# The beginning of a two-layer diffusion backbone: rows requested first, squared on ScalarE, and normalized beside the filter spectrum

## The chip, the cores and the metric

The kernel runs as one program on one core of a Trainium2 chip. A core has five engines with a queue of instructions each: TensorE (PE; its weight loads are listed as PEld), VectorE (DVE), ScalarE (ACT), GpSimd (POOL) and SyncE (SP). Each engine takes its own queue in order. SP does nothing but start transfers (DMA), and POOL starts others. The metric is the device time of one execution in microseconds (us), as the median of several.

## The reference

Two layers act on 1024 latent tokens and 256 context tokens of 1024 channels. Layer 0, cut to what matters here:

```python
sh1, sc1, g1, sh2, sc2, g2 = ada_mod(c, ada_w[i], ada_b[i])      # silu(c) @ w + b, six parts of 1024
u_lat = modulate(rms_norm(h_lat, norm1_g[i]), sh1, sc1)           # norm * (1 + sc1) + sh1
u_ctx = modulate(rms_norm(h_ctx, norm1_g[i]), csh1, csc1)
y_lat = mixer_ab(u_lat, *ab)      # p = u @ w_in; Fourier mixing of 512 channels, Hyena on the rest
h_lat = h_lat + g1 * y_lat
h_lat = h_lat + g2 * swiglu(modulate(rms_norm(h_lat, norm2_g[i]), sh2, sc2), ...)
```

Hyena's long convolutions use two filters for each sequence length. A small network (two sine layers) and a window make the raw filter, which is divided by the sum of its absolute values; then its spectrum is taken. None of that depends on the tokens, so filters, modulation and normalization are independent until the product with `w_in`. Layer 1 is a neighbourhood attention with a feed-forward part.

## The kernel before

Channels lie on the 128 partitions, tokens along the free axis: eight blocks (`b`) of channels, and pieces `pc` of 512 latent (0, 1) or 256 context tokens (2). Products keep float32 accuracy by splitting an operand into a rounded high and a low part (`split`: the high part is a copy on ACT, L349, the low one a subtraction on DVE, L351).

The program is written as Python generators that `run` advances in turn; each `next` emits some instructions. A planner then orders each engine's queue by its own simulated times, earlier-emitted work first where both could go. So the order of emission sets the order loosely, and the data and the free buffers set the rest. Tiles come from pools with a fixed number of buffers: 21 of 4 KB per partition (`S4`), 35 of 2 KB (`S2`), and small ones for temporaries and weights (`wh`, `wl`, `ws`, eight slots together for the matrices `mat`). A load into a pool is held in its queue until a buffer is free, and whatever stands behind it there waits too.

The generators of the beginning are:

- `filter_mlp`: the sine layers, on PE, DVE and ACT.
- `filter_raw` (`fr`): the third weight split (L696, L349, L351), then for each of four blocks the products on PE, multiplied on DVE by a window that SP has loaded (L720). It has three steps left when `run` comes to its loop over `fr`.
- `ada_first` (`ada1`): the first two of the six modulations (scale, then shift), as products of 16 weight tiles of 512 KB (`in_ada_k`, loaded by POOL). Eight tiles make the scale, eight the shift; each ends with a turn into columns (L514) and additions (L518, L521).
- `norms` (`ng`): ten loads of 512 KB rows of tokens (`in_x_row`), then the sum of squares of each row, then the root and its reciprocal, then a broadcast of the factors, then loads of the same tokens by channels (`in_ctx_t`, `in_x_t`, six ahead), then 24 blocks of `norm_block` (L623 on DVE, L625 on ACT, L626 on DVE). Odd rows are squared on DVE in one instruction with its sum, even rows on ACT.
- `spectrum_l`: eight steps for the first latent filter. It loads matrices (`in_ff_l`, by POOL), forms sums on DVE (L863 to L906), multiplies on PE and stores; `filter_sum` in it takes the absolute values (L745 to L749).

`in_proj` follows: 16 blocks of 128 outputs, each with a load of 512 KB of `w_in`, its split, 72 matmuls and, from the fifth, a short convolution on DVE (L978 to L982). Between blocks it advances other generators by a list of counts: the second filter, the context filters, and `late_groups`, in which modulations 2, 3 and 4 are made on DVE. One step of that (`ada_group`, 24 in all) loads two 256 KB halves of one weight block into `S2` buffers and reduces each against two conditionings (four instructions of L549, two of L551).

```python
for k, _ in enumerate(self.spectrum_l(0, raws["l"][0], self.cast_half)):
    if k < 3:
        next(ada1, None)
    else:
        drain(ada1)
    for _ in range(4):
        next(ng, None)
```

Of the kernel before, what the change touches and what calls it, by code (L numbers as in the profile page):

```python
# [10 lines left out]
F32 = mybir.dt.float32  # L11
F32R = mybir.dt.float32r
F16 = mybir.dt.float16
AF = mybir.ActivationFunctionType
ALU = mybir.AluOpType
AX = mybir.AxisListType.X
MUL, ADD, SUB, MAX, MIN = ALU.mult, ALU.add, ALU.subtract, ALU.max, ALU.min
# [241 lines left out]
class Builder:  # L259
# [273 lines left out]
    def ada_group(self, l, m, conds, where):  # L533

        nc, a = self.nc, self.a
        for nb in range(m * 8, m * 8 + 8):
            if where == "s2":
                st = [self.S2(), self.S2()]
                for j in (0, 1):
                    self.ld(st[j], a["ada_w"][l, nb, :, j * 512:(j + 1) * 512])  # L540
            else:
                t = self.mat(1024, F32) if where == "mat" else self.S4()
                (self.ld if where == "mat" else self.ldr)(t, a["ada_w"][l, nb])
                st = [t[:, :512], t[:, 512:]]
            for c in reversed(conds):
                half = self.pt.tile([P, 2], F32, tag="ah", name=self.nm("ah"))
                for j in (0, 1):
                    o = st[j] if c == 0 else self.T()
                    nc.vector.tensor_tensor_reduce(o, st[j], self.cond[c][j], 1.0, 0.0, MUL, ADD,  # L549
                                                   half[:, j:j + 1])  # L550
                nc.vector.tensor_tensor(self.ada[(l, c)][:, nb:nb + 1], half[:, 0:1], half[:, 1:2], ADD)  # L551
            yield
        sl = slice(m * 8, m * 8 + 8)
        for c in conds:
            t = self.ada[(l, c)]
            nc.vector.tensor_tensor(t[:, sl], t[:, sl], self.adab[:, l * 48 + m * 8:l * 48 + m * 8 + 8], ADD)
            if m in (1, 4):
                g = (0 if m == 1 else 2) + l
                nc.vector.scalar_tensor_tensor(t[:, sl], t[:, sl], 1.0, self.gs[:, g * 8:g * 8 + 8], op0=ADD, op1=MUL)
# [1813 lines left out]
    def run(self):  # L2373
        nc, a = self.nc, self.a
# [9 lines left out]
        def drain(g):  # L2384
            for _ in g:
                pass
# [3 lines left out]
        def norms():  # L2390
# [4 lines left out]
            yield  # L2395
            sq = self.C(10)
            for i, t in rows:
                if i % 2:
                    nc.vector.tensor_tensor_reduce(t, t, t, 1.0, 0.0, MUL, ADD, sq[:, i:i + 1])
                else:  # L2400
                    with self.follow(self.last_hi):
                        nc.scalar.activation(t, t, AF.Square, accum_out=sq[:, i:i + 1])
                yield
            nc.scalar.activation(sq, sq, AF.Sqrt, scale=1.0 / D, bias=self.eps)
            nc.vector.reciprocal(sq, sq)
# [1 line left out]
            for pc in PCS:  # L2407
                w = WID[pc]
                t = self.T()
                for j in range(w // P):  # L2410
                    i = OFF.get(pc, LAT) // P + j
# [31 lines left out]
        u = Act()  # L2443
        ng = norms()
# [3 lines left out]
        next(mlp)  # L2448
        next(fr)
        self.setup_late()  # L2450
        next(mlp)
        for _ in range(3):
            next(ada1)
# [2 lines left out]
            next(ada1)  # L2456
        with self.tc.issue_after(self.clamp), self.tc.issue_after(self.sin):
            next(fr)
        for _ in fr:
            next(ada1)  # L2460
        next(ng)
        for k, _ in enumerate(self.spectrum_l(0, raws["l"][0], self.cast_half)):
            if k < 3:
                next(ada1, None)
            else:
                drain(ada1)
            for _ in range(4):
                next(ng, None)
        self.held = True
        second = (x for g in (self.filter_raw("l", raws["l"], (1,)),  # L2470
                              self.spectrum_l(1, raws["l"][1], self.cast2)) for x in g)
        next(second)
        next(ng)
        next(second)
        drain(ng)
        ada = self.late_groups()
# [16 lines left out]
            yield from self.inverse_c(1, y)  # L2493

        fc, cc = four(), conv()
        self.in_proj(u, ((second, (3, 3, 3, 1)), (filt, (0,) * 7 + (2,)), (ada, (0, 0, 1) + (2,) * 11 + (1, 0))), fc, cc)
        self.held = False
        drain(second)
        drain(ada)
# [36 lines left out]
        u = None  # L2536
# [248 lines left out]
```

## Time and profile before

| what | value |
|---|---|
| median of 3 runs | 2913.51 us (2904.85 to 2915.74) |
| the profiled execution | 2907.72 us, span 2906.0 us |
| PE busy | 2785.5 us (96%) |
| DVE busy | 2070.6 us (71%) |
| ACT busy | 1312.4 us (45%) |
| mean rate of transfers | 193 GB/s |

The span is what the profile covers, from the first to the last instruction. A busy share is the time in which an engine had an instruction under way. A window's row gives, for one stretch of the span, its length, then for each engine the busy time and the number of instructions, then the granted clock of TensorE, the share of the transfer engines in use and the rate in GB/s. In the list of groups the last column is the idle time just before such instructions and what ended it. In the timeline the columns are start, duration, engine, line, operation, output and inputs, count, and in brackets the idle time before it. The list of waits gives for a waiter and a releaser the total, the number and the longest.

### The profile page before, as it was taken

The numbers are of one execution on the slowest core, as the hardware profiler recorded it, in microseconds if no ns is written. First come the engines' busy times: TensorE is split into PE (matmuls) and PEld (weight loads), VectorE is DVE, ScalarE is ACT, GpSimd is POOL, SyncE is SP. The second block draws the span as 40 slices with busy tenths as digits, with TensorE's granted clock in tenths as the row PEclk, the third lists the DMA queues.
The fourth block names the chain that finished last, engine by engine and source line by source line (L and its number), as shares of the span: only waits on it lengthen the run. The fifth ranks groups of instructions, "written<-read, shape, count | busy, mean of one in ns | idle before, by whom it ended". The sixth has DMA issues, their size and how long they took to land. (4 is left out here: it accounts for less than half of the span.)

```text
span 2906.0 us, 43708 instructions
## 1 busy us (share of the span) xinstructions
PE 2785.5 (96%) x15496; PEld 2329.1 (80%) x15496; DVE 2070.6 (71%) x3793; ACT 1312.4 (45%) x2253; POOL 535.5 (18%) x859
## 2 busy tenths in 40 slices
PE   7899898989999999999999999999999999999998
PEld 3587787778898888888888888888887788888886
DVE  6868797766787888966777536677678877764555
ACT  3433325443554333333455327777765443333433
POOL 2021134251011112222110002232221022111000
PEclk8899999999999999999999999999999999999999
DMA  8646445654556555659984436776856276434753
GB/s 295 202 146 188 156 154 176 212 185 163 201 186 207 191 199 195 224 183 330 310 308 150 138 128 152 178 194 180 244 187 216 89 256 224 153 109 160 237 189 131
DMA packets 302824, 561.54 MB, mean 193 GB/s; under 512 B 82568, under 2 KB 128842, under 8 KB 302606
## 3 DMA queue, kind: packets, MB, share of 16 engines
q1 hardware_dynamic: 241806, 375.73, 41.3%
q0 software_dynamic: 58496, 178.83, 17.4%
q10 hardware_dynamic: 2304, 4.20, 0.4%
q8 instruction: 122, 2.00, 0.3%
q14 instruction: 96, 0.79, 0.1%
HBM read 411.30 MB, written 119.80 MB: 183 GB/s over the span
## 5 line engine op out<-in xcount | busy, mean ns | idle before, releaser
L1796 PE MATMUL ps<-s,s 128*128 128x512 f32 x1956 | 483.6, 389 | 0.3 <-ACT s L349 0.3
L1796 PEld LDWEIGHTS ps<-s,s 128*128 128x128 f32 x1956 | 367.0, 188 | 77.6 <-ACT s L349 1.1
L345 PE MATMUL ps<-s,wh 128*128 128x256 f32 (+1 forms) x1684 | 386.5, 330 | 4.8 <-ACT wh L349 2.3
L345 PEld LDWEIGHTS ps<-s,wh 128*128 128x128 f32 x1684 | 285.3, 193 | 37.3 <-issue 3.0
L345 PE MATMUL pq<-s,wh 128*128 128x512 f32 (+1 forms) x940 | 287.7, 382 | 6.2 <-DVE s L2611 2.5
L351 DVE TENSOR_TENSOR wl<-ws,wh 128x1024 fp32r<-128x1024 f32 (+1 forms) x141 | 167.7, 1190 | 140.7 <-ACT wh L349 136.0
L1969 PE MATMUL ps<-s,s 128*128 128x512 f32 (+1 forms) x1000 | 259.8, 383 | 3.2 <-DVE s L351 3.1
L349 ACT CAST wh<-ws 128x1024 fp32r<-128x1024 f32 (+1 forms) x141 | 144.6, 1026 | 260.0 <-PE ps L345 139.8
L345 PE MATMUL ps<-s,wl 128*128 128x256 f32 (+1 forms) x842 | 259.8, 329 | 0.8 <-DVE wl L351 0.8
L349 ACT CAST s<-s 128x1024 fp32r<-128x1024 f32 (+2 forms) x188 | 170.2, 933 | 191.8 <-DMA s<-d 169.3
L345 PE MATMUL ps<-s,s 128*128 128x65 f16 (+4 forms) x2774 | 235.0, 238 | 17.8 <-ACT s L349 3.9
L351 DVE TENSOR_TENSOR s<-s,s 128x1024 fp32r<-128x1024 f32 (+2 forms) x166 | 188.2, 1164 | 53.6 <-ACT s L349 53.4
L1969 PEld LDWEIGHTS ps<-s,s 128*128 128x128 f32 x1000 | 184.4, 188 | 41.5 <-DVE s L351 5.1
L349 ACT CAST s<-t 128x512 fp32r<-128x512 f32 (+1 forms) x211 | 119.8, 583 | 207.0 <-PE ps L1796 68.4
L345 PEld LDWEIGHTS pq<-s,wh 128*128 128x128 f32 x940 | 171.3, 191 | 36.8 <-DVE s L626 2.8
L1796 PE MATMUL ps<-s,wh 128*128 128x512 f32 x600 | 187.9, 393 | 0.0
L351 DVE TENSOR_TENSOR s<-t,s 128x512 fp32r<-128x512 f32 (+1 forms) x211 | 135.8, 654 | 60.5 <-ACT s L349 36.7
L345 PE MATMUL pq<-s,wl 128*128 128x512 f32 (+1 forms) x470 | 178.1, 380 | 0.0
L345 PEld LDWEIGHTS ps<-s,wl 128*128 128x128 f32 x842 | 160.4, 192 | 16.7 <-DVE wl L351 1.0
L345 PEld LDWEIGHTS ps<-s,s 128*128 128x128 f32 (+1 forms) x854 | 131.0, 194 | 30.3 <-ACT s L349 5.2
L1969 PE MATMUL ps<-s 128*128 128x512 f32 (+1 forms) x500 | 150.6, 385 | 0.0
L336 POOL DMA_DIRECT2D d<-s x154 | 83.2, 542 | 355.2 <-DVE s L1605 112.8
(487 smaller groups left out, 5586.1 us busy)
## 6 DMA issues: line engine op xcount, KB each, us to landing
s<-d SPq DMA_DIRECT2D x283, 256.0 KB, 3.8
s<-in_down SPq DMA_DIRECT2D x150, 256.0 KB, 4.2
d<-s POOLq DMA_DIRECT2D x138, 256.0 KB, 3.5
s<-in_ada_w POOLq DMA_DIRECT2D x56, 512.0 KB, 5.0
d<-tk POOLq DMA_DIRECT2D x98, 256.0 KB, 4.2
ws<-in_up SPq DMA_DIRECT2D x44, 512.0 KB, 3.8
d<-g POOLq DMA_DIRECT2D x86, 256.0 KB, 3.2
ws<-in_gate SPq DMA_DIRECT2D x42, 512.0 KB, 3.7
```

The costliest lines, as they stand in the source:

```text
L336: self.last_ldr = self.nc.gpsimd.dma_start(out, in_).ins
L345: self.nc.tensor.matmul(o, l, r, start=st, stop=sp)
L349: self.last_hi = nc.scalar.copy(hi, src).ins
L351: self.last_lo = eng.tensor_tensor(lo, src, hi.bitcast(F32), SUB).ins
L1796: nc.tensor.matmul(ps, x[:, sl], y, start=first and j == 0 and x is wh and y is xh, stop=j == 3 and x is wl, skip_group_check=True)
L1969: m = nc.tensor.matmul(acc[j][:, c0:c1], x[:, sl], y[:, xs], start=first and k == 0, stop=last and k == 2, skip_group_check=True)
```

## The change

`ada_group` gets an inner function that loads one weight block. In the `s2` form (the one of `late_groups`) the first block of a group is loaded before the loop and each step loads the next block before it reduces its own; the other forms load as they did. In `norms` all ten rows are squared on ACT. In `run` the row loads are emitted right after `setup_late`, the first modulation is emitted whole ahead of the spectrum, and the row squares and later steps of `norms` are spread over the loop over `fr` (two each) and the spectrum (three for each of its steps, where four were). In `in_proj` the counts for `late_groups` begin at the first block (1, 1, 1, then nine times 2, then 1, 1, 1, 0) where they were 0, 0, 1, then eleven times 2, then 1, 0.

```diff
     def ada_group(self, l, m, conds, where):
         nc, a = self.nc, self.a
-        for nb in range(m * 8, m * 8 + 8):
+        def load(nb):
             if where == "s2":
                 st = [self.S2(), self.S2()]
                 for j in (0, 1):
                     self.ld(st[j], a["ada_w"][l, nb, :, j * 512:(j + 1) * 512])
-            else:
-                t = self.mat(1024, F32) if where == "mat" else self.S4()
-                (self.ld if where == "mat" else self.ldr)(t, a["ada_w"][l, nb])
-                st = [t[:, :512], t[:, 512:]]
+                return st
+            t = self.mat(1024, F32) if where == "mat" else self.S4()
+            (self.ld if where == "mat" else self.ldr)(t, a["ada_w"][l, nb])
+            return [t[:, :512], t[:, 512:]]
+
+        ready = [load(m * 8)] if where == "s2" else []
+        for nb in range(m * 8, m * 8 + 8):
+            if where != "s2" or nb < m * 8 + 7:
+                ready.append(load(nb + len(ready)))
+            st = ready.pop(0)
             for c in reversed(conds):
...
             for i, t in rows:
-                if i % 2:
-                    nc.vector.tensor_tensor_reduce(t, t, t, 1.0, 0.0, MUL, ADD, sq[:, i:i + 1])
-                else:
-                    with self.follow(self.last_hi):
-                        nc.scalar.activation(t, t, AF.Square, accum_out=sq[:, i:i + 1])
+                with self.follow(self.last_hi):
+                    nc.scalar.activation(t, t, AF.Square, accum_out=sq[:, i:i + 1])
                 yield
...
         self.setup_late()
+        next(ng)
         next(mlp)
...
-        for _ in fr:
+        for i, _ in enumerate(fr):
             next(ada1)
-        next(ng)
+            for _ in range(2 if i < 5 else 1):
+                next(ng)
+        drain(ada1)
         for k, _ in enumerate(self.spectrum_l(0, raws["l"][0], self.cast_half)):
-            if k < 3:
-                next(ada1, None)
-            else:
-                drain(ada1)
-            for _ in range(4):
+            for _ in range(3):
                 next(ng, None)
...
         next(second)
-        next(ng)
+        next(ng, None)
         next(second)
...
-        self.in_proj(u, ((second, (3, 3, 3, 1)), (filt, (0,) * 7 + (2,)), (ada, (0, 0, 1) + (2,) * 11 + (1, 0))), fc, cc)
+        self.in_proj(u, ((second, (3, 3, 3, 1)), (filt, (0,) * 7 + (2,)), (ada, (1, 1, 1) + (2,) * 9 + (1, 1, 1, 0))), fc, cc)
```

`follow(x)` puts the instructions of its block behind `x` in their engine's queue; `last_hi` is the latest high copy of `split` emitted by then.

## The prediction

> **What bounds the kernel now.** I read the page's engine shares first, then the table by windows with borders at the ends of the stages that the change touches, then for each stage the groups with the idle time before them and the timeline.
>
> ```profile
> span 2906.0 us, 43708 instructions
> PE 2785.5 (96%) x15496; PEld 2329.1 (80%) x15496; DVE 2070.6 (71%) x3793; ACT 1312.4 (45%) x2253; POOL 535.5 (18%) x859
> ...
> 21.00:50.00 29.00, 25.12 (x73) 10.94 (x71) 17.21 (x33) 4.75 (x9) 3.77 (x8) 0.82 1.06 401
> ...
> 53.00:76.00 23.00, 12.33 (x32) 6.74 (x31) 23.00 (x33) 19.57 (x31) 1.05 (x2) 0.72 0.37 125
> 76.00:91.00 15.00, 15.00 (x50) 9.41 (x50) 3.68 (x14) 6.70 (x16) 0.00 (x0) 0.74 0.11 36
> 91.00:141.00 50.00, 39.11 (x156) 27.73 (x156) 49.92 (x85) 24.67 (x43) 3.18 (x6) 0.86 0.81 267
> 141.00:180.00 39.00, 36.94 (x205) 31.64 (x204) 20.81 (x42) 10.63 (x22) 6.95 (x9) 1.00 0.31 104
> 180.00:340.00 160.00, 145.34 (x739) 120.97 (x738) 130.01 (x354) 56.62 (x118) 29.17 (x46) 0.96 0.56 178
> 340.00:460.00 120.00, 109.96 (x553) 92.20 (x551) 101.70 (x247) 35.57 (x65) 32.49 (x35) 0.94 0.47 147
> 460.00:2906.00 2446.00, 2381.82 (x13659) 2024.32 (x13658) 1712.56 (x2972) 1148.97 (x1945) 448.87 (x730) 0.99 0.60 194
> ```
>
> TensorE bounds the kernel as a whole: from 460 us on it is busy 2381.82 of 2446 us. So an edit ahead of 460 us is worth what it brings forward the point from which TensorE runs full, and time won there is kept behind it. The stages ahead have other limits. From 21 to 50 us the transfer engines are full (share 1.06, 401 GB/s). From 53 to 76 VectorE is busy every microsecond, from 91 to 141 for 49.92 of 50. Between them, from 76 to 91, it does 3.68 us of work. From 141 to 180 TensorE is the limit with 36.94 of 39. From 180 to 460, the rest of `in_proj`, TensorE idles 14.7 + 10.0 us and VectorE 30.0 + 18.3 us, and neither is the limit by itself: they wait for each other.
>
> **The change part by part.** First the rows, which are requested ahead of the windows now.
>
> ```profile
> 5.10 0.79 SPq L330 DMA_DIRECT2D c<-in_ada_b  x1
> ...
> 8.77 10.60 SPq L330 DMA_DIRECT2D s<-in_win_l  x8
> 20.89 16.08 SPq L330 DMA_DIRECT2D s<-in_x_row  x10
> ...
> s<-in_x_row SPq DMA_DIRECT2D x10, 512.0 KB, 12.4
> mat<-in_ff_l POOLq DMA_DIRECT2D x8, 512.0 KB, 4.7
> s<-in_win_l SPq DMA_DIRECT2D x8, 256.0 KB, 12.5
> ...
> 52.65 0.69 DVE L720 TENSOR_TENSOR s<-ps,s 128x512 f32<-128x512 f32 x1
> 54.93 1.88 PE L345 MATMUL ps<-mat,c 128*2 128x512 f32 x4
> ...
> L720 DVE TENSOR_TENSOR s<-ps,s 128x512 f32<-128x512 f32 x12 | 7.6, 682 | 10.3 <-PE ps L345 10.3
> ```
>
> SP's queue holds the two in the other order after the change. From the end of `in_ada_b` at 5.9 us the ten rows take 16.1 us to issue, to 22, and the last lands 12.4 us later, at 34. The eight windows, moved behind ten transfers, take 10.6 us more, to 32.6, and the last lands at 45.1. Its product (L720, 0.69 us) then ends near 46. Before, the last product ended at 53.3, not for want of windows but because VectorE waited 10.3 us for TensorE (its biggest wait in L720's main group, up to 53 us). TensorE's queue has the shift's weight tiles among the filter's products, and POOL could not load the last of those tiles while matrices of the spectrum held the slots. Emitted whole ahead of the spectrum, those tiles go ahead of the spectrum's matrices in POOL's queue. So the raw filter is complete 7 us earlier. Ends: 0, if the products still stand behind late tiles, and 10.3, the whole wait. I take 7, by the sum of issue and landing.
>
> The moved spectrum matrices have the price of a stall at worst of one landing, 4.7 us (the median of `in_ff_l` up to 110 us), and nothing if they land before the raw filter is complete; they are hidden by the 46 us that the other transfers need anyway. I take 0.
>
> A rule of the Trainium skill bears on this (DMA: Bandwidth & Descriptors, sections "Queues, rings and completion order" and "Issuing engines are not separate DMA queues"). Transfers of all issuing engines share the same 16 transfer engines, which take turns between the queues packet by packet. The full share of 1.06 agrees. By it SP's queue would have half of the rate while POOL's has work, and with an estimated 8.2 MB up to the last window at half of 401 GB/s would end at 41 instead of 45 us. It also speaks against the edit: order is all that the change alters, not the rate.
>
> ```profile
> L2399 DVE CUSTOM_DVE_ANT_0 s<-s 128x1024 f32<-128x1024 f32 x5 | 6.1, 1215 | 0.0
> L2402 ACT ACTIVATE s<-s 128x1024 f32<-128x1024 f32 x5 | 5.2, 1050 | 0.0
> L2402 ACT ACTIVATION_READ_ACCUMULATOR s<-s 128x1 f32 x5 | 0.9, 188 | 0.0
> ACT s L349 <- DVE tk L873: 23.2, 1, 23.2
> ```
>
> Second, the squares. Five leave VectorE, 5 x 1.215 = 6.1 us out of the full stretch around 53 to 76. Ten on ScalarE take 10 x (1.050 + 0.188) = 12.4 us. ScalarE idled 23.2 us in one piece ahead of the spectrum's first cast, which waited for sums (L873) of the spectrum, and with the rows landing up to 34 us the squares fit into that gap. What stands behind them in ScalarE's queue are the absolute values of the raw filter, which cannot begin before some products are done. Cost 0; if the rows landed 10 us later than worked out, the 12.4 us would end some 10 us into the spectrum's work and delay the absolute values by up to 4. The ends are -6.1 and +4; I take -6.
>
> Third, the hole in VectorE's work from 76 to 91.
>
> ```profile
> 86.12 6.26 SPq L330 DMA_DIRECT2D ws<-in_w_in  x3
> ...
> 90.80 1.23 DVE L351 TENSOR_TENSOR wl<-ws,wh 128x1024 fp32r<-128x1024 f32 x1 [5.70 <-ACT wh L349]
> 92.43 1.37 SPq L330 DMA_DIRECT2D s<-in_ctx_t  x3
> 94.41 0.23 DVE L518 TENSOR_TENSOR c<-ps,c 128x8 f32<-128x8 f32 x2
> ...
> 100.84 1.66 DVE L623 SCALAR_TENSOR_TENSOR t<-s,c,s 128x256 f32<-128x256 f32 x4
> ```
>
> VectorE idles there because the next things in its queue are not ready: the split of `w_in` (5.70 us, SP requested it only from 86.12 on), and the spectrum's sums, which follow. The 24 normalized blocks would have filled the hole, but the shift's columns came only at 94.41, the tokens by channels were requested at 92.43, and the first block starts at 100.84. In the changed order the row factors are ready some 30 us earlier, the shift too, and the blocks are emitted beside the spectrum's last steps. The hole is 15 - 3.68 = 11.3 us. Filled wholly it moves the end of the blocks by 11.3, not at all by 0. I take 5: the row of the split shows that a queue in order keeps such waits even where other work is ready.
>
> These three make 7 + 6 + 5 = 18 us at the end of the blocks (141 us before). TensorE has to take it up: it was busy 39.11 of 50 us from 91 to 141, partly at a granted clock of 0.86, so 10.9 us of its idle time there are free, and the rest must come from the idle time of 53 to 76 (10.7 us). I count 14 of the 18 as kept. Ends: 0 and the sum of the upper ends, 10.3 + 6.1 + 11.3 = 27.7.
>
> Fourth, the later modulations.
>
> ```profile
> L549 DVE CUSTOM_DVE_ANT_0 t<-s,s 128x512 f32<-128x512 f32 x48 | 37.1, 787 | 31.2 <-DMA s<-in_ada_w 28.7 <-ACT s L530 2.3
> L549 DVE CUSTOM_DVE_ANT_0 s<-s,s 128x512 f32<-128x512 f32 x48 | 35.0, 730 | 0.0
> L551 DVE TENSOR_TENSOR c<-ah 128x1 f32<-128x1 f32 x48 | 9.4, 199 | 0.1
> L549 DVE DVE_READ_ACCUMULATOR2_ANT ah<- 128x1 f32 x96 | 7.6, 79 | 0.0
> ...
> PE ps L345 <- DVE s L351: 5.4, 1, 5.4
> PE ps L345 <- DVE s L980: 3.5, 2, 2.5
> PE ps L345 <- DVE s L982: 2.8, 2, 2.0
> PE pq L345 <- DVE s L351: 2.4, 1, 2.4
> ```
>
> Over 180 to 460 us VectorE stood 28.7 us for the weight blocks, because each was requested in the step that reduces it. Splits and convolutions that TensorE needs stand behind that wait. Requested one step ahead, the loads land (about 5 us) during other work; what is left is the first step of each of the three groups, some 3 waits of the kind (28.7 over 15 waits, seen one by one, is 1.9 us each): 5.7 us. So 23 us of VectorE's 48.3 idle us in this stage, about half, go. TensorE's waits for VectorE in the fence sum to 14.1; half of it is 7, and I take 6. Ends: 0 and 14.1.
>
> A step costs VectorE (37.1 + 35.0 + 9.4 + 7.6)/24 = 3.7 us. Two steps move from the thirteenth and fourteenth block of `in_proj` to the first two: 7.4 us. If they land between 141 and 180, 18.2 idle us of VectorE cover them; if they land ahead of 141, in the full stretch, they cost up to 7.4, and they give up to as much back at the end. I take 0, ends -7.4 and +7.4. The prefetch holds two more of the 35 `S2` buffers, and the four with the conditionings are taken two blocks earlier; what that may do stands with the rivals.
>
> **Sum**: 2907.72 - 14 - 6 = 2887.7 against the profiled execution. The median of the three runs, 2913.51, lies 5.8 above it, which gives 2893.5. I predict the middle, 2890 us.
>
> **Rivals.**
>
> *The order gives nothing.* The first 50 us are bound by transfers whose bytes are the same; the windows are later by as much as the rows are earlier, and VectorE's blocks still follow the spectrum because its matrices or the tokens by channels arrive late. For it: the 401 GB/s, and the product of the last window at 46 us, later than the first three quarters of the products before. Against it: 11.3 us of hole and the 6.1 us off VectorE do not depend on transfers. Then only the squares and half of the fourth part are left, 6 + 3 = 9 us: about 2902.
>
> *The edit does little of what it says*: the planner takes what is ready by its own times, and places blocks and prefetched loads nearly where they were. For it: the shift's last products ran at 54.93 us, amid the spectrum, though they are emitted in its later steps. Then the time is that of before, 2910.
>
> *The buffers: slower.* An earlier load that waits for an `S2` buffer holds SP's queue, and the load of `w_in` is behind it.
>
> ```profile
> SPq L330 <- DVE wl L351: 55.9, 10, 11.8
> ...
> ws<-in_w_in SPq DMA_DIRECT2D x4, 512.0 KB, 5.1
> ...
> 130.20 0.33 SPq L330 DMA_DIRECT2D ws<-in_w_in  x1
> ...
> 141.84 1.05 ACT L349 CAST wh<-ws 128x1024 fp32r<-128x1024 f32 x1
> ```
>
> `w_in` was requested at 130.20 and used at 141.84; with 5.1 us to land it had 6.5 us to spare. SP's longest such wait up to 330 us is 11.8 us. A hold of that length costs TensorE 11.8 - 6.5 = 5.3 us for a block. With seven of the fifteen blocks that carry steps the price is 37 us, against 14 gained: 2907.7 + 37 - 14 = 2931. It decides from six blocks on (6 x 5.3 = 32, above 14 + 14.6). Against it: the planner starts a load when it believes a buffer free, and the hold needs it to be wrong again and again. In a sentence beside it: the Trainium skill (Perfetto Trace Analysis, "Optimization Strategy") reads a gap that repeats on the engine that should be full as a sign that buffers ran out; no run here shows it yet.
>
> **How the numbers follow.** Forecast 0.45 (2872 to 2902); the order gives nothing 0.22 (2898 to 2908); little of what it says 0.13 (2905 to 2917); the buffers 0.20 (2920 to 2945). From no change a measurement tells about 0.5%, 14.6 us, so faster is under 2899 and slower above 2928. Faster: nearly all of the first and a little of the second, 0.47. Slower: most of the last, 0.18, and some room for a planner's order that goes wrong later, 0.03 more. Same: the rest, 0.32. The range is 2868 (the sum with 27.7 and 14.1, 2866, is nearly its lower end) to 2928; what it leaves out is most of the last rival and a few in a hundred below. The forecast's own range is 2872 to 2902.
>
> **What would show it.** Ten squares on ScalarE between 25 and 45 us and none on VectorE; last L720 near 46 instead of 53.3; L518's second pair near 50 instead of 94; the first L623 before 90 and the last L626 near 125 instead of 141; VectorE busy more than 11 of 15 us where the hole was; the wait of L549 for `in_ada_w` under 8 us; the span from the end of `in_proj` on unchanged. Wrong it would be if the absolute values wait behind squares, if the first L623 still starts near 100, or if SP shows waits above 12 us ahead of `w_in` loads in the first blocks of `in_proj`.

## The result and the profile after

The change makes no difference that the measurement can tell: 2909.23 us against 2909.84 us (medians of 12 executions each), a ratio of 1.0001 with a 95% interval of 0.9989 to 1.0013. The forecast of 2890 us was wrong. The profiled execution took 2911.94 us, its span 2910.2 us.

The table by windows of the kernel after, with the borders of the prediction (length, busy time of TensorE, its weight loads, VectorE, ScalarE and POOL with counts, granted clock, share of the transfer engines, GB/s):

```profile
21.00:50.00 29.00, 16.65 (x44) 9.62 (x44) 11.16 (x22) 23.08 (x45) 1.06 (x2) 0.66 0.87 344
53.00:76.00 23.00, 21.25 (x56) 6.87 (x55) 16.99 (x23) 7.95 (x12) 4.23 (x8) 0.95 0.59 183
76.00:91.00 15.00, 14.79 (x54) 10.43 (x53) 6.92 (x15) 5.04 (x11) 0.00 (x0) 0.71 0.39 132
91.00:141.00 50.00, 33.26 (x126) 24.08 (x127) 48.21 (x86) 24.48 (x42) 3.18 (x6) 0.80 0.68 222
141.00:180.00 39.00, 33.64 (x174) 28.04 (x173) 28.06 (x64) 14.04 (x28) 6.96 (x8) 0.96 0.55 189
180.00:340.00 160.00, 145.91 (x732) 120.74 (x732) 124.89 (x324) 53.50 (x111) 28.14 (x45) 0.94 0.54 171
340.00:460.00 120.00, 115.05 (x586) 96.63 (x586) 100.76 (x250) 37.54 (x68) 30.65 (x36) 0.97 0.44 138
```

VectorE did 17.21 us of work from 21 to 50 before and does 11.16 now. From 53 to 76, where it was full before, it is idle 6 of 23 us. VectorE's work has moved later, not earlier. Its timeline says why (start, duration, engine, line, operation, output and inputs, count, and in brackets the idle time before and what ended it; lines behind `ada_group` stand 7 higher than before, so L727 is the old L720, L630 and L633 the old L623 and L626):

```profile
43.76 0.22 DVE L2409 RECIPROCAL c<-c 128x10 f32<-128x10 f32 x1 [17.46 <-ACT c L2408]
43.89 0.64 DVE L727 TENSOR_TENSOR s<-ps,s 128x512 f32<-128x512 f32 x1
...
58.88 1.29 DVE L727 TENSOR_TENSOR s<-ps,s 128x512 f32<-128x512 f32 x2 [7.94 <-PE ps L345]
...
68.69 1.28 DVE L727 TENSOR_TENSOR s<-ps,s 128x512 f32<-128x512 f32 x2
...
80.26 0.24 DVE L518 TENSOR_TENSOR c<-ps,c 128x8 f32<-128x8 f32 x2 [1.34 <-PE ps L345]
87.23 0.88 DVE L630 SCALAR_TENSOR_TENSOR tk<-s,c,s 128x256 f32<-128x256 f32 x2 [6.73 <-DMA s<-in_ctx_t]
...
142.96 0.74 DVE L633 SCALAR_TENSOR_TENSOR s<-t,c,s 128x512 fp32r<-128x512 f32 x1
```

The reciprocal of the row factors stands in VectorE's queue ahead of the first product of the raw filter and waits 17.46 us for ScalarE. The first product starts at 43.89 (31.02 before, the line below), the last pair at 68.69 (52.65). The blocks begin at 87.23, as forecast ahead of 90, but the last one ends at 143.7 (141.1 before). In the kernel before:

```profile
31.02 0.69 DVE L720 TENSOR_TENSOR s<-ps,s 128x512 f32<-128x512 f32 x1 [2.92 <-PE ps L345]
```

The other three queues of the beginning in the kernel after, ScalarE, SP and TensorE, one after the other:

```profile
25.24 1.05 ACT L2406 ACTIVATE s<-s 128x1024 f32<-128x1024 f32 x1
...
40.02 1.06 ACT L2406 ACTIVATE s<-s 128x1024 f32<-128x1024 f32 x1 [1.37 <-DMA s<-in_x_row]
40.98 0.19 ACT L2406 ACTIVATION_READ_ACCUMULATOR s<-s 128x1 f32 x1
41.07 1.04 ACT L511 COPY g<-ps 2x512 f32<-2x512 f32 x2
42.12 1.28 ACT L2408 ACT_TABLE_LOAD   x1
```

```profile
6.37 14.48 SPq L330 DMA_DIRECT2D s<-in_x_row  x10
23.04 0.33 SPq L330 DMA_DIRECT2D c<-in_skip  x1
25.53 0.33 SPq L330 DMA_DIRECT2D c<-in_conv  x1
28.02 14.11 SPq L330 DMA_DIRECT2D s<-in_win_l  x8
83.73 0.33 SPq L330 DMA_DIRECT2D d<-s  x1
84.11 0.43 SPq L330 DMA_DIRECT2D s<-in_ctx_t  x1
```

```profile
41.68 2.08 PE L345 MATMUL ps<-s,s 128*128 128x512 f32 x4 [7.56 <-ACT g L511]
...
50.15 8.03 PE L345 MATMUL ps<-mat,c 128*2 128x512 f32 x14
...
75.50 2.93 PE L345 MATMUL ps<-s,mat 128*128 128x512 f32 x6
```

The ten squares run on ScalarE from 25.24 to 41.2, as forecast, but the copies of the first modulation (L511), the table for the root and the root itself stand behind them, and TensorE waits 7.56 us for those copies. SP issues nothing from 42.1 to 83.73: the token loads stand behind stores of the spectrum, and the spectrum's first product on TensorE comes at 75.50 (53.34 before). The waits of VectorE for ScalarE's `w_in` copies and for the modulation's weights, from 180 to 460 us (total, number, longest), before and after:

```profile
DVE t L549 <- DMA s<-in_ada_w: 28.7, 15, 6.9
DVE wl L351 <- ACT wh L349: 8.4, 4, 2.9
```

```profile
DVE wl L351 <- ACT wh L349: 22.1, 9, 6.4
DVE t L556 <- DMA s<-in_ada_w: 14.0, 8, 5.1
```

14.7 us of the wait for the weights went and 13.7 us of the wait for the copies came.

### The profile page after: what moved, and what is told of

It reads as the page before. It is cut to its first block, busy times and chain, and to the rows that moved or that the text cites. A ratio compares the mean times of both kernels' runs of the same rounds, so it can differ in the third digit from the quotient of the medians.

```text
span 2910.2 us, 43750 instructions
## 1 busy us (share of the span) xinstructions
PE 2787.2 (96%) x15496; PEld 2330.4 (80%) x15496; DVE 2063.2 (71%) x3783; ACT 1319.1 (45%) x2263; POOL 534.7 (18%) x859
## 5 line engine op out<-in xcount | busy, mean ns | idle before, releaser
L345 PEld LDWEIGHTS ps<-s,wh 128*128 128x128 f32 x1684 | 286.6, 193 | 37.1 <-issue 4.0
L1976 PEld LDWEIGHTS ps<-s,s 128*128 128x128 f32 x1000 | 184.6, 188 | 41.1 <-DVE s L351 4.5
L351 DVE TENSOR_TENSOR s<-t,s 128x512 fp32r<-128x512 f32 (+1 forms) x214 | 137.8, 655 | 60.6 <-ACT s L349 35.9
```

Of the source, the lines that this page charges most:

```text
L345: self.nc.tensor.matmul(o, l, r, start=st, stop=sp)
L351: self.last_lo = eng.tensor_tensor(lo, src, hi.bitcast(F32), SUB).ins
L1976: m = nc.tensor.matmul(acc[j][:, c0:c1], x[:, sl], y[:, xs], start=first and k == 0, stop=last and k == 2, skip_group_check=True)
```

## The experiments

Nothing of the computation is left out in any of them. Every time is a median; ratios are to the kernel before on the same chip, with 95% intervals. From each trace five marks are read, in us: the first and the last product of the raw filter and the first spectrum product (their starts), the end of the last normalized block, and the first turn of the inverse stage (the start of the first matmul of L1159, L1166 with the new `ada_group`), which stands where `in_proj` ends.

| kernel | first, last product | first spectrum product | last block ends | first turn | us | ratio |
|---|---|---|---|---|---|---|
| before | 31.0, 52.7 | 53.3 | 141.1 | 462.0 | | 1 |
| the change | 43.9, 68.7 | 75.5 | 143.7 | 469.7 | 2909.23 | 1.0001 (0.9989 to 1.0013) |
| late_only | 31.1, 52.8 | 53.5 | 141.2 | 465.8 | 2906.10 | 0.9997 (0.9986 to 1.0007) |
| begin_only | 42.5, 67.4 | 74.1 | 142.1 | 468.4 | 2908.85 | 1.0005 (0.9994 to 1.0017) |
| prefetch_only | 31.6, 53.5 | 54.2 | 142.0 | 462.9 | 2903.37 | 0.9985 (0.9977 to 0.9994) |
| squares_only | 31.8, 51.1 | 51.8 | 137.8 | 460.5 | 2902.06 | 0.9986 (0.9977 to 0.9995) |
| squares_prefetch | 31.1, 50.3 | 51.3 | 136.8 | 459.8 | 2907.65 | 1.0001 (0.9991 to 1.0011) |
| rows_first_only | 40.8, 64.4 | 66.6 | 155.3 | 479.6 | 2919.71 | 1.0041 (1.0026 to 1.0056) |
| drain_only | 31.8, 54.4 | 55.0 | 141.1 | 465.9 | 2909.82 | 1.0008 (0.9996 to 1.0020) |
| begin_root_late | 41.1, 68.3 | 72.2 | 141.4 | 466.9 | 2907.59 | 0.9997 (0.9988 to 1.0006) |
| windows_first | 33.0, 55.2 | 78.7 | 145.7 | 475.1 | 2917.38 | 1.0031 (1.0019 to 1.0042) |
| windows_tokens | 32.3, 54.6 | 78.1 | 136.2 | 466.8 | 2907.97 | 1.0002 (0.9992 to 1.0012) |
| windows_prefetch | 33.1, 55.4 | 78.9 | 145.7 | 472.1 | 2918.18 | 1.0038 (1.0025 to 1.0052) |
| factors_behind | 31.4, 56.5 | 57.2 | 138.2 | 461.3 | 2901.14 | 0.9972 (0.9961 to 0.9983) |
| after_factors_behind | 44.2, 67.9 | 69.2 | 143.4 | 462.6 | 2908.69 | 1.0006 (0.9997 to 1.0015) |
| factors_prefetch | 33.0, 55.6 | 56.3 | 137.3 | 458.9 | 2901.24 | 0.9989 (0.9975 to 1.0003) |

### The two halves

late_only is the kernel before with the new `ada_group` and the new counts of `in_proj`; begin_only is the changed kernel with both as before.

```diff
-            else:
...
+        ready = [load(m * 8)] if where == "s2" else []
...
-        self.in_proj(u, ((second, (3, 3, 3, 1)), (filt, (0,) * 7 + (2,)), (ada, (0, 0, 1) + (2,) * 11 + (1, 0))), fc, cc)
+        self.in_proj(u, ((second, (3, 3, 3, 1)), (filt, (0,) * 7 + (2,)), (ada, (1, 1, 1) + (2,) * 9 + (1, 1, 1, 0))), fc, cc)
```

> The kernel before, with the weight blocks of the later modulations loaded one step ahead and their steps begun at the first block of the input projection; the beginning is as it was. Theory A (two halves of opposite sign: the late part gains, the beginning loses as much): VectorE's wait for these blocks falls from 28.7 to about 14 us, the first turn of the inverse stage comes at about 452 to 456 us instead of 461.8, and the time falls by 6 to 10 us against the kernel before. Theory B (neither half does anything that reaches the end; VectorE's waits only change their names): the turn comes within 3 us of 461.8 and the time within 3 us.

> The changed beginning alone (rows first, all squares on ScalarE, first modulation emitted whole, normalization spread), with the later modulations as before. Theory A: VectorE stands some 17 us ahead of the reciprocal of the row roots with the filter's products queued behind it, the first spectrum matmul comes near 75 us instead of 53, the first turn of the inverse stage at about 470 to 477 us instead of 461.8, and the time rises by 6 to 13 us. Theory B: the turn within 3 us of 461.8 and the time within 3 us.

Measured: neither half changes the time by what the measurement can tell (0.9997 and 1.0005). So it is not a gain of one half that the other cancels. In both traces the first turn comes later than before, by 3.8 and 6.4 us, and the times do not show it. Each half was taken apart.

### The later half: the prefetch alone

prefetch_only has the new `ada_group` and the old counts.

> Only the load one step ahead; the steps are spread over the input projection as before. If the load ahead carries the gain of the late part (theory A1), the wait falls to about 14 us and the time is within 2 us of that of the late part alone. If the earlier begin of the steps carries it (A2), the time is within 2 us of the kernel before.

Measured: 0.9985, about 4 us, where late_only, with the earlier counts, has 0.9997. VectorE's wait for the weights falls to 10.6 us. These are its longest waits from 180 to 460 us now:

```profile
DVE wl L351 <- ACT wh L349: 23.9, 7, 7.6
DVE t L556 <- DMA s<-in_ada_w: 10.6, 5, 5.1
DVE s L351 <- DMA d<-s: 4.1, 1, 4.1
```

The three make 38.6 us; before, the two of the first fence above made 37.1. So VectorE hardly waits less, it waits for something else: the high copy of `w_in` above all. TensorE's busy time from 180 to 460 us rises by 1.1 us (146.45 + 109.99 against 255.30). The 4 us of the median are real by the interval, but the trace of one execution does not show where they arise. The earlier counts bring no gain of their own, and with them this one is gone.

### The beginning: one part at a time

squares_only squares all rows on ScalarE and changes nothing else; squares_prefetch adds the new `ada_group` to it.

```diff
-                if i % 2:
-                    nc.vector.tensor_tensor_reduce(t, t, t, 1.0, 0.0, MUL, ADD, sq[:, i:i + 1])
-                else:
-                    with self.follow(self.last_hi):
-                        nc.scalar.activation(t, t, AF.Square, accum_out=sq[:, i:i + 1])
+                with self.follow(self.last_hi):
+                    nc.scalar.activation(t, t, AF.Square, accum_out=sq[:, i:i + 1])
```

> The kernel before with all ten row squares on ScalarE and nothing else. If VectorE's work from 53 to 76 us sets the pace there (as I forecast), 6 us less of it brings the first normalized block from 100.8 to about 95 us and the time falls by 3 to 6 us. If what sets the pace there is the arrival of operands for TensorE and the order of the queues, ScalarE, busy 19.6 of 23 us in that stretch, becomes the limit with 6 us more, and the time stays within 3 us or rises.

> The two parts that gained by themselves, together: all squares on ScalarE and the load one step ahead, with the order of emission and the counts as before. If the two are independent the time falls by 4.3 + 3.7, near 8 us (ratio 0.997). If the planner's order is what made each of them gain, the sum is less, 2 to 5 us.

Measured: the squares alone bring 0.9986 and end the blocks 3.3 us earlier. Together with the prefetch they bring nothing (1.0001), though the blocks end a further 1.0 us earlier. Two gains of 0.15%, each beyond its interval, do not add.

rows_first_only requests the rows ahead of the windows and leaves the rest as before.

```diff
         self.setup_late()
+        next(ng)
         next(mlp)
...
-        next(ng)
         for k, _ in enumerate(self.spectrum_l(0, raws["l"][0], self.cast_half)):
```

> The kernel before with the row loads emitted ahead of the windows and nothing else; odd rows are squared on VectorE as before. Theory D: the windows land 10 us or more later and the products with them, first product near 40 us instead of 31, the first turn 2 to 5 us later than 461.8. Theory C: without the reciprocal in front of the products the later windows cost nothing at the end; the first turn within 2 us of 461.8.

Measured: slower by 0.41%, about 12 us. The first product starts 9.8 us later, the last 11.8, the first spectrum product 13.3, the last block ends 14.2 later and the first turn comes 17.6 later. But the late windows are not the only cause. The odd rows are still squared on VectorE, and the planner put these squares among the sine layers of `filter_mlp`, where VectorE waits 11.6 us for rows:

```profile
21.16 1.22 DVE L2399 CUSTOM_DVE_ANT_0 s<-s 128x1024 f32<-128x1024 f32 x1 [9.06 <-DMA s<-in_x_row]
...
38.17 1.29 DVE L351 TENSOR_TENSOR s<-t,s 128x512 fp32r<-128x512 f32 x2
...
40.78 0.69 DVE L720 TENSOR_TENSOR s<-ps,s 128x512 f32<-128x512 f32 x1 [0.16 <-DMA s<-in_win_l]
```

The weight split of the raw filter comes at 38.17 (26.80 before), and the first product waits only 0.16 us more for its window. So this run does not price the late windows by themselves.

drain_only ends the first modulation ahead of the spectrum.

```diff
+        drain(ada1)
         for k, _ in enumerate(self.spectrum_l(0, raws["l"][0], self.cast_half)):
-            if k < 3:
-                next(ada1, None)
-            else:
-                drain(ada1)
```

> The kernel before with the first modulation emitted whole ahead of the spectrum and nothing else. If its place matters, the shift's columns come well before 94 us and the first normalized block before 98 instead of 100.8, with the time 2 to 4 us lower. If what holds the blocks is the request of the tokens by channels, the first block stays at 100 us or later and the time within 2 us.

Measured: nothing (1.0008). The last of its 16 weight tiles is requested at 24.2 us (49.3 before), the second pair of L518 comes at 63.19 instead of 94.41, and the first block still starts at 100.85 (100.84 before). So the blocks had not waited for the shift's columns. And TensorE shows what the products had waited for. VectorE's longest wait for it in the kernel before, TensorE in that kernel, and TensorE in drain_only:

```profile
46.46 2.48 DVE L720 TENSOR_TENSOR s<-ps,s 128x512 f32<-128x512 f32 x4 [7.41 <-PE ps L345]
```

```profile
36.53 9.23 PE L345 MATMUL ps<-mat,c 128*2 128x512 f32 x18
```

```profile
36.26 8.75 PE L345 MATMUL ps<-mat,c 128*2 128x512 f32 x20
44.93 1.20 PE L345 MATMUL ps<-s,s 128*128 128x512 f32 x4
```

With its weights long requested, the modulation still holds TensorE for 8.75 us (9.23 for 18 such products before), and VectorE's waits for TensorE in this group sum to 11.0 us (10.3 before). So the wait of 7.41 us was for TensorE's own work, not for late tiles.

### Where the chain of row factors stands

The row factors need rows, squares on ScalarE, a table load and a root there, the reciprocal on VectorE, diagonals on ScalarE and a broadcast on TensorE. begin_root_late is begin_only with the reciprocal placed behind the products in VectorE's queue.

```diff
-                        nc.vector.tensor_tensor(t, ps, w, MUL)
+                        self.last_raw = nc.vector.tensor_tensor(t, ps, w, MUL).ins
...
-            nc.vector.reciprocal(sq, sq)
+            with self.follow(self.last_raw):
+                nc.vector.reciprocal(sq, sq)
```

> The changed beginning alone, with one more order: the reciprocal of the row roots stands behind the latest product of the raw filter in VectorE's queue. Theory C (the reciprocal, queued ahead of the products, is what delays the beginning): VectorE's wait of 14.9 us goes, the first product starts before 38 us, the first spectrum matmul comes near 65 us instead of 74, the first turn of the inverse stage near 461 instead of 468.4. Theory D (the windows, issued behind the rows, and the scale's copies, queued behind the squares on ScalarE, hold the products anyway): the first product still starts after 40 us and the first turn stays within 3 us of 468.4.

Its VectorE timeline:

```profile
41.08 0.69 DVE L720 TENSOR_TENSOR s<-ps,s 128x512 f32<-128x512 f32 x1 [13.81 <-DMA s<-in_win_l]
```

The first product now waits for a window instead, until 41.08. In begin_only, the kernel to compare with, the reciprocal waits 14.95 us and the first product starts at 42.48. So the wait for the root covered one for the window that is nearly as long: the reciprocal by itself costs 42.48 - 41.08 = 1.4 us there, the rest is the windows. Theory D holds; the last product (68.3) is no earlier than in begin_only, and the time stays (0.9997).

So the windows were given back. windows_first leaves the order of the loads as before and emits 13 steps of `norms` (loads, squares, root, broadcast) between the products and the spectrum; windows_tokens emits 14, so that the first six token loads are requested ahead of the spectrum's stores; windows_prefetch adds the new `ada_group`.

```diff
-        for _ in fr:
+        for i, _ in enumerate(fr):
             next(ada1)
-        next(ng)
+        for _ in range(13):
+            next(ng)
+        drain(ada1)
...
-            for _ in range(4):
+            for _ in range(3):
                 next(ng, None)
```

> The changed beginning alone, with one part undone: the rows are requested behind the windows again, as in the kernel before (so their squares, all on ScalarE, are emitted behind the raw filter too); the first modulation is still whole ahead of the spectrum and the normalization spread beside it. Theory E (the request of the rows ahead of the windows is what takes the rest of the change's gain): the first product comes near 31 us and the last near 54, as before; the first normalized block near 85 us, the last near 130 instead of 141, and the time falls by 5 to 10 us. Theory F (the other parts gain nothing that TensorE can use, whatever the order of the requests): the last block within 4 us of 141 and the time within 4 us.

> The same, and the first tokens by channels are requested one emission step earlier, ahead of the spectrum's first stores in SP's queue. If the stores in front of these requests are what holds the normalized blocks (VectorE waited 6.6 us for them in the changed beginning), the first block comes another 8 us or more earlier and the time falls by 2 to 4 us more. If the blocks wait for the shift's columns or the row factors, both stay as in the run without it.

> The changed beginning with the windows first, and the weight blocks of the later modulations loaded one step ahead with the counts as before: the parts of the change that did not lose. If gains of the beginning and of the load ahead add, the time is 3 to 4 us below that of the run without the load ahead. If, as with the squares, they do not, it is the same or higher.

Measured: windows_first is slower by 0.31%, against every expectation of it. Its products are nearly on time (33.0 to 55.2), but the spectrum comes at 78.7. TensorE and VectorE show the new hold:

```profile
71.93 1.22 PE L345 MATMUL pq<-t,c 128*128 128x256 f32 x2 [16.76 <-ACT t L2409]
73.10 2.08 PE L345 MATMUL pq<-tk,c 128*128 128x512 f32 x2
```

```profile
70.88 0.22 DVE L2402 RECIPROCAL c<-c 128x10 f32<-128x10 f32 x1 [4.33 <-ACT c L2401]
71.01 0.63 DVE L863 TENSOR_TENSOR t<-s 128x512 f32<-128x512 f32 x1
```

The broadcast of the factors stands ahead of the spectrum on TensorE and waits 16.76 us; on VectorE the spectrum's first sums (L863, at 37.02 before) stand behind the reciprocal. Requesting the tokens ahead of the stores (windows_tokens) brings the end of the blocks from 145.7 to 136.2 and the ratio from 1.0031 to 1.0002, with the spectrum still at 78.1: the token loads behind the stores are a second hold. The prefetch brings nothing here (1.0038).

factors_behind moves only the chain: 11 steps (loads and squares) ahead of the spectrum, the root and all that follows from its second step on.

```diff
-        for _ in range(13):
+        for _ in range(11):
             next(ng)
         drain(ada1)
         for k, _ in enumerate(self.spectrum_l(0, raws["l"][0], self.cast_half)):
-            for _ in range(3):
+            for _ in range(3 if k else 0):
                 next(ng, None)
```

> windows_first with one thing moved: ahead of the spectrum stand only the ten row loads and the ten squares (eleven steps of the normalization); the root, the broadcast and everything behind them are emitted from the spectrum's second step on, three steps to each. The filter's windows, the shift tiles ahead of the spectrum and the order of the loads stay as in windows_first. Theory Q (the chain of row factors, emitted ahead of the spectrum, is what holds the spectrum in the queues of ACT, DVE and PE): the first product of the spectrum on PE comes back from 78.72 us to between 53 and 60, the reciprocal no longer stands on DVE ahead of the spectrum's sums, and the time is 5 to 12 us below that of windows_first, 2905 to 2912 us, a ratio to before of 0.999 to 1.0015. Rival R (not the factors: the squares on ACT, or the shift tiles emitted ahead of the spectrum, hold it): the first product of the spectrum stays behind 70 us and the ratio stays near 1.003. Rival S (the spectrum comes back but the time does not follow it, because the tokens requested behind the spectrum's stores hold the last blocks): first product of the spectrum under 60, last normalized block still at 144 to 147 us, ratio still near 1.003.

Measured: 0.9972, 16 us below windows_first and 8 us below before; the two intervals are far apart. The spectrum is back at 57.16, the reciprocal stands at 75.38 among the spectrum's splits and waits 0.92 us, the blocks start at 83.39 and end at 138.2, and the first turn comes 13.8 us earlier than in windows_first (461.3 against 475.1). Theory Q holds, and the gain is larger than it said. The stretch from 53 to 91 us, windows_first and then factors_behind:

```profile
53.00:91.00 38.00, 18.21 (x72) 10.60 (x70) 20.65 (x36) 24.35 (x47) 1.06 (x2) 0.77 0.35 117
```

```profile
53.00:91.00 38.00, 28.23 (x99) 16.40 (x98) 25.86 (x47) 32.25 (x59) 1.60 (x4) 0.87 0.49 161
```

Each of the three engines does more in the same 38 us, TensorE 10.0 us more. factors_behind has the lowest ratio of all kernels here (its interval meets those of squares_only and prefetch_only), and it has three ideas of the change in it: all squares on ScalarE, the first modulation emitted whole ahead of the spectrum, and the blocks started beside the spectrum.

after_factors_behind moves the chain in the changed kernel itself; factors_prefetch adds the new `ada_group` to factors_behind.

```diff
-            for _ in range(2 if i < 5 else 1):
+            for _ in range(2 if i < 3 else 1):
                 next(ng)
...
-            for _ in range(3):
+            for _ in range(3 if k else 0):
                 next(ng, None)
```

> The changed kernel with one thing moved: of the normalization only the ten squares are emitted beside the window products; the root, the broadcast and everything behind them are emitted from the spectrum's second step on, three steps to each. The rows are still requested ahead of the filter's windows and still squared on ScalarE, the first modulation still ends ahead of the spectrum, its prefetch and the later counts stay. Theory Q2 (two holds in series: the rows in front of the windows put the last product near 66, and the chain of row factors adds the rest): the first product starts near 41 and waits for a window, the last product starts at 65 to 68, the first spectrum product on PE comes at 66 to 70 instead of 75.5, and the time is 2 to 7 us below that of the change, a ratio to before of 0.9975 to 0.9993; the 4 to 8 us that are missing to factors_behind are the price of the rows asked for first. Rival R2 (the chain of factors holds everything): the first spectrum product comes back under 60 and the ratio is 0.997, like factors_behind. Rival R3 (the chain costs nothing where the windows are late): the ratio stays at 0.9995 to 1.001.

> factors_behind with the change's new order of requests for the modulation's weights (the next tile requested ahead of the work on this one) and nothing else; the counts of the planner are those of before. If the gains add, the prefetch alone having given a ratio of 0.9985 and factors_behind 0.9972, the ratio to before is 0.9950 to 0.9963 (2894 to 2898 us). If they do not, as with the squares and the prefetch together (1.0001) and windows_first with and without it (1.0031 and 1.0038), the ratio is 0.9968 to 0.9990. The wait of DVE for the modulation's weights falls from 24.5 us to 10 to 14 in either case.

Measured: after_factors_behind has the marks of theory Q2 (last product 67.9, spectrum 69.2) but the time of R3 (1.0006). So where the windows are late, moving the broadcast brings the spectrum 6.3 us forward, the first turn 7.1 us (462.6 against 469.7), and the time nothing that the measurement can tell. By its trace the chain does cost something there; why the time does not follow stays open. One part of the edit did not act: the planner put the reciprocal, emitted later, ahead of the products all the same.

```profile
44.10 0.22 DVE L2409 RECIPROCAL c<-c 128x10 f32<-128x10 f32 x1 [18.21 <-ACT c L2408]
44.23 0.64 DVE L727 TENSOR_TENSOR s<-ps,s 128x512 f32<-128x512 f32 x1
```

By begin_root_late that is worth some 1.4 us, the rest of that wait being windows. factors_prefetch has 0.9989 with an interval that overlaps that of factors_behind: a gain of the prefetch does not show there either. It also gives the nearest price of the rows requested first. It was measured beside after_factors_behind, both have the chain behind and the prefetch, and they differ in the request of the rows, in the squares emitted between the products, and in the counts: 2901.24 against 2908.69, 7.5 us, with intervals that overlap a little.

## Why the prediction was wrong

**First term, the raw filter 7 us earlier: this is the step that failed.** It came 16 us later. The sum of issues and landings put the last window at 45.1 us, and the transfer engines were in fact full until about 45 us. But that was luck: SP issued the windows from 28.02 to 42.1 and not from 22 to 32.6, and the last but one then landed in 4.4 us and not in 12.5. Two things around the sum were wrong. I asked when the last window lands and not when the first does: VectorE takes them in order, and by begin_root_late the first product has to wait until 41 us for a window that it had at 31 before. And I read VectorE's 10.3 us of waiting for TensorE as late weight tiles. It was the modulation's own products: drain_only requests the tiles 25 us earlier and the wait stays, and in the changed kernel it is 7.94 us, now behind a start at 50.15 instead of 36.53. The price of the rows requested first, with the earlier counts in it, is 7.5 us (after_factors_behind against factors_prefetch), a loss where a gain of 7 was summed.

On the page rule weighed there (the Trainium skill, DMA: Bandwidth & Descriptors, "Queues, rings and completion order"): by the estimate from it, half of the rate for SP's queue, the last window would have been in at 41 us. It was issued only at 41.7. That the transfer engines take turns between the queues agrees with the shares moved: over the first 60 us POOL's queue moved 9.01 MB and SP's 8.24 MB.

**Second term, the squares, -6 on VectorE and 0 on ScalarE.** Alone it brought about 4 us, right in sign and near in size. In the changed kernel the 0 was wrong. I named the absolute values as what stands behind the squares; between the two stood the modulation's copies (L511, at 41.07 instead of 22) and the root. TensorE waited 7.56 us for those copies, until 41.68, and the rest of the modulation's products came behind that. And I missed a part of the change: the text ahead of the prediction says that three steps of `fr` are left at its loop. There are seven (four blocks of two windows, less the one taken). So all squares, the root and the broadcast, twelve steps of `norms`, are emitted ahead of the last products, and not six squares. Likewise the first modulation was emitted to its last three steps before the spectrum already, so "drained ahead" changes little. Counting the yields would have shown both.

**Third term, the hole, 5 of 11.3 us.** VectorE does 6.92 us there and not 11; the blocks began 13.6 us earlier as foreseen, and ended 2.6 later. What was late next I had not named: the token loads (6.73 us of waiting at 87.23), requested at 84.11 behind a store of a spectrum that was itself 22 us late. Blocks and spectrum share VectorE, which is busy 48.21 of 50 us from 91 to 141, so it stands to reason that an early start of the one is paid by the other; no run here separates the two.

The chain of row factors in front of the spectrum, in three queues, was in none of my terms. It is what windows_first against factors_behind measures: 16 us. The Trainium skill has the rule (PSUM — Partial Sum Buffer, section "Engine vs sequencer instructions": the queues of ScalarE, VectorE and GpSimd are strictly first in, first out, and TensorE's matmuls start in program order). The 17.46 us on VectorE and the 16.76 us on TensorE agree with it, and by factors_behind, where the spectrum begins at 57.16, it could have run during the second. The prediction had even the sentence that says it ("a queue in order keeps such waits"), but used it only to shrink a gain.

The costs are not additive. With the windows late, the chain waits beside them: begin_only has both and 1.0005, windows_first only the second and 1.0031, factors_behind neither and 0.9972. With both, the chain is done at 43.8 us in the change, little later than the first window is in; with the windows on time, its squares mix with the absolute values on ScalarE and it is done at 71.

**Fourth term, the prefetch, 6 us.** Alone it brought about 4, near its size, but not by the mechanism: the wait for the weights fell to 10.6 us (14.0 in the change) and not to 5.7, and a wait for ScalarE's copies took its place almost us for us. With the earlier counts, priced at 0 with ends of 7.4, the gain is gone (late_only).

**The premise that time won ahead of 460 us is kept** holds only roughly. Over the 16 kernels, with one trace each, the end of the last block and the ratio go together, 0.9 us of time for each us (a straight line through the table, which leaves 3.4 us of scatter and covers 60% of the spread). For the first turn it is 0.8 us, 2.9 us and 71%. In the change the blocks ended 2.6 us later and the first turn came 7.7 us later, at no cost that the medians show. factors_behind reaches the turn only 0.7 us ahead of the kernel before and is 8 us faster. So a part of these differences arises behind the turn, which I had taken as unchanged: from there to the end of the span the 16 traces need 2436.8 to 2444.0 us, and the kernel before needs the most.

**The rivals.** "The order gives nothing" came nearest in mechanism: the windows late by as much as the rows are early, blocks behind the tokens. Its 2902 kept 9 us for squares and prefetch, which in the change came to nothing. "Little of what it says" had the time, 2910, for the wrong reason: the planner did move what was emitted earlier. "The buffers: slower" did not happen: SP's longest wait for a split of `w_in` from 180 to 460 us is 15.4 us against 14.7 before.

**What stays open.** Why gains of 0.15% do not add (squares_prefetch, factors_prefetch), where the prefetch's 4 us arise, and why the change loses 7.7 us ahead of the first turn and nothing in the end. One trace for each kernel shows stages that differ by a few us in either direction with every new order of the planner, and no run here tells such an effect from the edit's own. A rival for the small differences is the clock. The granted clock of TensorE, as a mean over a kernel's executions, was 0.9816 for factors_behind and 0.9791 for the kernel before beside it, 0.9815 against 0.9795 for squares_only, but 0.9784 against 0.9800 for after_factors_behind. If all of TensorE's 2785.5 busy us went by it, the first pair would make 7 us and the last 4.6 (estimates). No run tells whether the order of the work moves this clock. So the 8 us of factors_behind against the kernel before may not all be the edit's own; of its 16 us against windows_first, 13.8 stand in the traces already at the first turn.

## What to carry to other kernels

An instruction emitted early is not free because its engine is idle: with queues in order it stands in front of everything emitted after it, so for each part of a chain that is moved forward ask when its last input arrives, on every engine that it passes, and what stands behind it there. Price a moved transfer by the first of the delayed loads, not by the last. And before an idle time is put down to a late transfer, look at whether the engine waited for was simply busy. The same holds for the time that a queue takes to issue its loads: look at what each issue waited for.

## What the runs showed that was not expected

SP's queue takes 0.3 to 0.5 us to issue a load that waits for nothing. In the changed kernel, behind ten loads of 512 KB and with POOL's queue busy too, two loads of 4 and 24 KB and the first window started 2.5 us apart (23.04, 25.53, 28.02; the same in rows_first_only, 23.66, 26.14, 28.64), the rows took 17.1 us to land instead of 12.4, and 7.2 us passed between the last row's issue and the first window's. The list of SP's waits in the kernel after, from 5 to 30 us, says what held it (total, number, longest):

```profile
SPq L330 <- DMA s<-in_x_row: 10.7, 5, 2.2
```

Each of these loads waits in the program for a semaphore, and eight semaphores serve the loads of this queue in turn. In the trace each of the three starts 0.02 us after the load eight places ahead of it, a row, had landed (at 23.02, 25.51 and 28.00). So no more than eight loads of SP are under way at once in this stretch. A large load moved forward then delays the ones behind it by its landing, and not only by its own issue. This is also why SP's times of issue in the kernel before, which the prediction's sum took over, did not hold in the new order: they were times of landing.
